# Scores of a 64-row head contracted over 128 rows, with each head's queries in zero-padded tiles of their own

## The chip, the cores and the metric

One Trainium2 chip; the kernel is one program on one of its cores. The metric is device time in microseconds of one execution, the median of several. The core's engines are named as in the profile: PE (TensorE matmul), PEld (TensorE weight load), DVE (VectorE), ACT (ScalarE), POOL (GpSimd) and SP (SyncE, which issues the transfers).

## The reference, cut to what matters

The model is one decoder layer over 512 tokens of width 1024: a half-step SwiGLU, a token mixing part, a cross-attention into 256 memory tokens, a second half-step SwiGLU, a final norm. The change lies in the token mixing part, whose mixer B is a causal attention with 8 heads of 64 channels, each query seeing keys by three strides:

```
q = z[..., o0:o0 + D_ATT].reshape(b, s, N_HEADS, HEAD_DIM)      # 8 heads of 64
k = z[..., o0 + D_ATT:o0 + 2 * D_ATT].reshape(b, s, N_HEADS, HEAD_DIM)
...
scores = jnp.einsum('bnqrhe,bnkrhe->bnrhqk', qb.astype(F32), kb.astype(F32)) * (e ** -0.5)
```

A score is a sum over the 64 channels of one head. Two heads fill the 128 rows of one tile.

## The kernel before, in words

All matrix products are made to float32 accuracy out of three products of a rounded half and a rest (`mm3`, lines 124 to 129: high by high on L127, high by low on L128, low by high on L129). So each operand exists as a pair of tiles, `...H` and `...L`, which `split` (L102 to L104) makes: ACT copies to the rounded tile (L103) and DVE subtracts (L104). Such pairs of 128 x 512 tiles come from one pool of 40 buffers (`h_tile`, L96). PSUM has four buffers for accumulators (`acc`) and four for everything short (`aux`).

In the mixing part (`mixers`, L389 on) the projections run as `z_block`, each 96 matmuls of 512 columns. Queries and keys come out with tokens on the rows; `qk_transpose` (L438) turns them with PE transposes (L442) into four tiles per call, two of queries and two of keys, and splits each to `qkH` and `qkL`. Tile m holds head 2m in rows 0 to 63 and head 2m+1 in rows 64 to 127. The call with b = 0 stands ahead of the last projection, the one with b = 1 in the middle of the attention.

The attention works on 32 units (tile m, half r, block i of 128 queries). For a unit u three functions are called at different steps: `scores(u)` (L491: one `mm3` on the 64 rows of the half r, over 256, 256, 384 or 512 keys, then DVE adds the mask and takes the maximum on L501, ACT takes the exponent on L505, DVE scales by the reciprocal sum on L508 and L509), `transposes(u - 3)` (L512: PE transposes on L517, then a split to the `pt` pair; one block of `pt` is zero-filled by POOL on L524), and `values(u - 4)` (L530: matmuls of `pt` by the value tiles, then ACT and DVE make `yH` and `yL`, L548 and L549). A unit of attention matmuls is short, so the work that the mixer's output projection can already do (`mix_out`, L607, part 0: 96 matmuls `acc<-yH` and `acc<-yL` on the other mixer's half) stands among the units as filler.

The order on each engine is not written out by hand: the program is traced, and a scheduler puts each engine's instructions in one fixed order by priorities and its own estimates. Engines keep that order and wait for each other by semaphores.

Of the kernel before, what the change touches and what calls it, by code (L numbers as in the profile page):

```python
# [24 lines left out]
P = 128  # L25
# [29 lines left out]
def body(tc, I, out):  # L55
    nc = tc.nc
    from contextlib import ExitStack
    ctx = ExitStack()
    with ctx:
# [22 lines left out]
        ps = paux.tile([P, S], F32, name="warm_ps", tag="aux")  # L82
# [10 lines left out]
        def aux_tile():  # L93
            return paux.tile([P, S], F32, name="aux", tag="aux")

        def h_tile(n):  # L96
            return hp.tile([P, S], F32R, name=n, tag="h")

        def f32(ap):
            return ap.bitcast(F32)  # L100

        def split(hi, lo, src):  # L102
            ins = nc.scalar.activation(hi, src, AF.Copy)  # L103
            nc.vector.tensor_sub(lo, src, f32(hi))  # L104
            return ins
# [14 lines left out]
        def at(x, i):  # L120

            return x[i[0]][i[1:]] if isinstance(x, list) and isinstance(i, tuple) else x[i]

        def mm3(ps, a, b, ia, ib, start, stop):
            aH, aL = at(a[0], ia), at(a[1], ia)
            bH, bL = at(b[0], ib), at(b[1], ib)
            nc.tensor.matmul(ps, lhsT=aH, rhs=bH, start=start, stop=False)  # L127
            nc.tensor.matmul(ps, lhsT=aH, rhs=bL, start=False, stop=False)  # L128
            nc.tensor.matmul(ps, lhsT=aL, rhs=bH, start=False, stop=stop)  # L129
# [259 lines left out]
        def mixers(norm, cs):  # L389
            col = []  # L390
            hshape = [P, 8, 64]
            with tc.tile_pool(name="mix", bufs=1) as mp:
# [43 lines left out]
                qT, kT = {}, {}  # L436

                def qk_transpose(b):  # L438
                    for m in range(4):
                        ps = aux_tile()  # L440
                        for t in range(NT):
                            nc.tensor.transpose(ps[:, t * P:(t + 1) * P],  # L442
                                                qk[t][:, m * P:(m + 1) * P], ident_b)
                        hi, lo = h_tile("qkH"), h_tile("qkL")
                        split(hi, lo, ps)
                        (qT if m < 2 else kT)[2 * b + m % 2] = (hi, lo)

                vH = [h_tile("vH") for _ in range(NT)]
                vL = [h_tile("vL") for _ in range(NT)]
# [7 lines left out]
                z_block(norm, 2, qk_evac)  # L457
                z_block(norm, 3, v_evac)
                qk_transpose(0)


# [14 lines left out]
                for t in range(NT):  # L476
                    vt = V[:, t].rearrange("p (g c) -> p g c", g=8)
                    r = rs[:, t * 8:(t + 1) * 8]
# [11 lines left out]

                def scores(u):  # L491
                    m, r, i = units[u]
                    rows = slice(r * 64, (r + 1) * 64)
                    n = (i + 1) * P
                    N = max(n, 256)
                    sc = aux_tile()
                    mm3(sc[:, :N], qT[m], kT[m], (rows, slice(i * P, (i + 1) * P)),
                        (rows, slice(0, N)), True, True)
                    s = mp.tile([P, S], F32, name="s", tag="s2", bufs=SB)
                    nmx = sm.tile([P, 1], F32, name="nmx", tag="nmx")  # L500
                    nc.vector.tensor_tensor_reduce(  # L501
                        out=s[:, :n], in0=sc[:, :n], in1=const[:, C_MASK + S - n:C_MASK + S],
                        scale=-ATT_SCALE, scalar=3e38, op0=ALU.add, op1=ALU.min, accum_out=nmx)
                    Z = sm.tile([P, 1], F32, name="Z", tag="Z")
                    nc.scalar.activation(s[:, :n], s[:, :n], AF.Exp, bias=nmx, scale=-1.0,  # L505
                                         accum_out=Z)
                    rz = sm.tile([P, 1], F32, name="rz", tag="rz")
                    nc.vector.reciprocal(rz, Z)  # L508
                    nc.vector.tensor_scalar_mul(s[:, :n], s[:, :n], rz)  # L509
                    prob[u] = s  # L510
# [80 lines left out]
                for u in range(LAG):  # L591
                    scores(u)
                z_block(norm, 4, qk_evac)
                gate_out()
                for u in range(LAG, nu + LAG + 1):
                    if u == nu // 2 - LAG - 1:
                        qk_transpose(1)
                    if u < nu:
                        scores(u)
                    transposes(u - LAG) if u - LAG < nu else None  # L600
                    if u > LAG:
                        values(u - LAG - 1)
# [281 lines left out]
```

## Time and profile before

| | |
|---|---|
| time, median of 3 runs | 1136.86 us (1136.83 to 1137.74) |
| the profiled execution | 1139.12 us |
| its span, first to last instruction | 1137.3 us |
| PE busy | 1121.1 us (99% of the span) |
| PEld busy | 936.4 us (82%) |
| DVE busy | 589.2 us (52%) |
| ACT busy | 422.6 us (37%) |
| POOL busy | 66.2 us (6%) |
| mean granted TensorE clock | 0.993 of full speed |
| stage with the scores | first score matmul at 468.7 us, last at 555.2 us |

PE is busy nearly throughout, so what a stage costs is mostly how closely its matmuls follow each other. A matmul's end is modelled in this profile and neighbours overlap on paper; the time that a matmul takes from the stream is the distance of its start from the next one's start. That distance, and not the duration shown, is used below.

### The profile page before, as it was taken

What the parts mean: (1) busy time and instruction counts of PE and PEld (TensorE: products, weight loads), DVE (VectorE), ACT (ScalarE), POOL (GpSimd) and SP (SyncE); (2) the same over time, 40 slices, a digit from 0 to 9 for tenths busy, and PEclk for the clock granted to TensorE, in tenths of its full rate; (3) what the DMA queues carried; (4) which work ended last, traced back from release to release, by engine and by line L of the source; (5) the groups of instructions that cost most, each with busy time, mean ns of one, the idle gap of its engine ahead of it and who ended that gap; (6) DMA issues with size and microseconds to landing.
All of it is one profiled execution on the core that took longest, in us unless ns stands there. A gap on an engine that the chain in (4) does not pass through costs nothing. (4 is left out here: it accounts for less than half of the span.)

```text
span 1137.3 us, 13932 instructions
## 1 busy us (share of the span) xinstructions
PE 1121.1 (99%) x5472; PEld 936.4 (82%) x5472; DVE 589.2 (52%) x1023; ACT 422.6 (37%) x668; POOL 66.2 (6%) x82
## 2 busy tenths in 40 slices
PE   9999999999999999999999999999999999999996
PEld 7788888888888888877868988778888888888996
DVE  4544533444344456578797555455444334445542
ACT  6332322332233433567655344433222222233420
POOL 2000100000002000001121000120000000000011
PEclk9999999999999999999989999999999999999998
DMA  6322333222233423010135412132232333323511
GB/s 218 112 93 88 114 97 128 93 93 94 83 88 114 141 93 108 25 45 29 41 111 196 165 63 74 47 102 93 95 99 75 89 125 97 108 93 113 154 63 38
DMA packets 39698, 110.79 MB, mean 97 GB/s; under 512 B 4432, under 2 KB 9296, under 8 KB 39632
## 3 DMA queue, kind: packets, MB, share of 16 engines
q1 hardware_dynamic: 39632, 109.89, 30.1%
q8 instruction: 43, 0.70, 0.2%
q14 instruction: 23, 0.19, 0.1%
HBM read 107.78 MB, written 2.10 MB: 97 GB/s over the span
## 5 line engine op out<-in xcount | busy, mean ns | idle before, releaser
L103 ACT ACTIVATE whi<-wraw 128x1024 fp32r<-128x1024 f32 (+2 forms) x213 | 202.8, 953 | 522.0 <-PE acc L128 300.9
L104 DVE TENSOR_TENSOR wlo<-wraw,whi 128x1024 fp32r<-128x1024 f32 (+2 forms) x213 | 238.4, 1120 | 166.7 <-ACT whi L103 166.4
L127 PE MATMUL acc<-hH,whi 128*128 128x512 f32 x768 | 300.8, 392 | 0.6 <-ACT hH L202 0.6
L128 PE MATMUL acc<-hL,whi 128*128 128x512 f32 x768 | 299.3, 390 | 0.8 <-DVE hL L203 0.8
L129 PE MATMUL acc<-hH,wlo 128*128 128x512 f32 x768 | 299.3, 390 | 0.5 <-DVE wlo L104 0.5
L128 PEld LDWEIGHTS acc<-hL,whi 128*128 128x128 f32 x768 | 144.3, 188 | 31.6 <-DVE hL L203 1.5
L127 PEld LDWEIGHTS acc<-hH,whi 128*128 128x128 f32 x768 | 144.3, 188 | 31.6 <-ACT hH L202 1.0
L129 PEld LDWEIGHTS acc<-hH,wlo 128*128 128x128 f32 x768 | 144.2, 188 | 30.6 <-DVE wlo L104 1.0
L127 PE MATMUL acc<-hidH,whi 128*128 128x512 f32 (+1 forms) x308 | 115.5, 375 | 0.0
L129 PE MATMUL acc<-hidH,wlo 128*128 128x512 f32 (+1 forms) x308 | 115.3, 374 | 0.0
L128 PE MATMUL acc<-hidL,whi 128*128 128x512 f32 (+1 forms) x308 | 115.3, 374 | 0.0
L170 POOL TENSOR_TENSOR sq<-sq 128x512 f32<-128x512 f32 (+1 forms) x39 | 49.3, 1265 | 778.8 <-ACT sq L178 778.4
L247 DVE TENSOR_TENSOR u<-acc,R 128x512 f32<-128x512 f32 x44 | 30.4, 690 | 121.6 <-PE acc L129 121.6
L243 DVE TENSOR_TENSOR gp<-acc,R 128x512 f32<-128x512 f32 x44 | 30.4, 691 | 85.6 <-PE acc L129 81.7
L128 PEld LDWEIGHTS acc<-hidL,whi 128*128 128x128 f32 x308 | 58.0, 188 | 10.3
L127 PEld LDWEIGHTS acc<-hidH,whi 128*128 128x128 f32 x308 | 58.0, 188 | 10.2
L129 PEld LDWEIGHTS acc<-hidH,wlo 128*128 128x128 f32 x308 | 58.0, 188 | 10.2
L127 PE MATMUL acc<-whi,hH 128*128 128x512 f32 x160 | 62.6, 391 | 0.0
L129 PE MATMUL acc<-whi,hL 128*128 128x512 f32 x160 | 62.4, 390 | 0.0
L128 PE MATMUL acc<-wlo,hH 128*128 128x512 f32 x160 | 62.3, 389 | 0.0
L230 DVE SCALAR_TENSOR_TENSOR x<-acc,x 128x512 f32<-128x512 f32 (+1 forms) x40 | 23.3, 584 | 75.0 <-PE acc L129 75.0
L178 ACT ACTIVATE sq<-x 128x512 f32<-128x512 f32 (+1 forms) x48 | 26.0, 551 | 41.8 <-DVE x L230 39.2
(211 smaller groups left out, 1476.6 us busy)
## 6 DMA issues: line engine op xcount, KB each, us to landing
wraw<-up SPq DMA_DIRECT2D x44, 512.0 KB, 3.5
wraw<-gate SPq DMA_DIRECT2D x43, 512.0 KB, 3.4
wraw<-down SPq DMA_DIRECT2D x28, 384.0 KB, 3.1
wraw<-w_in SPq DMA_DIRECT2D x20, 512.0 KB, 3.5
wraw<-down SPq DMA_DIRECT2D x28, 320.0 KB, 2.8
wraw<-w_out SPq DMA_DIRECT2D x16, 256.0 KB, 2.6
wraw<-wv SPq DMA_DIRECT2D x8, 512.0 KB, 3.4
wraw<-wk SPq DMA_DIRECT2D x8, 512.0 KB, 4.0
```

The costliest lines, as they stand in the source:

```text
L103: ins = nc.scalar.activation(hi, src, AF.Copy)
L104: nc.vector.tensor_sub(lo, src, f32(hi))
L127: nc.tensor.matmul(ps, lhsT=aH, rhs=bH, start=start, stop=False)
L128: nc.tensor.matmul(ps, lhsT=aH, rhs=bL, start=False, stop=False)
L129: nc.tensor.matmul(ps, lhsT=aL, rhs=bH, start=False, stop=stop)
L170: nc.gpsimd.tensor_add(self.parts[0], self.parts[0], sq)
L178: nc.scalar.activation(sq, src, AF.Square)
L230: nc.vector.scalar_tensor_tensor(X[d][:, tok], acc, 0.5, X[d][:, tok], op0=ALU.mult, op1=ALU.add)
L243: nc.vector.tensor_mul(gp, ps[0], R)
L247: nc.vector.tensor_mul(u, ps[1], R)
```

## The change

Keys stay as they are: two heads in one tile. Queries get, for each of the two heads, a pair of tiles of their own, whose other 64 rows POOL fills with zeros; ACT and DVE split only the head's own 64 rows into it. The score matmuls then take all 128 rows of the query tile and of the key tile; the rows of the other head meet zeros.

```
@@ -441,9 +441,21 @@
                         for t in range(NT):
                             nc.tensor.transpose(ps[:, t * P:(t + 1) * P],
                                                 qk[t][:, m * P:(m + 1) * P], ident_b)
-                        hi, lo = h_tile("qkH"), h_tile("qkL")
-                        split(hi, lo, ps)
-                        (qT if m < 2 else kT)[2 * b + m % 2] = (hi, lo)
+                        if m >= 2:
+                            hi, lo = h_tile("qkH"), h_tile("qkL")
+                            split(hi, lo, ps)
+                            kT[2 * b + m % 2] = (hi, lo)
+                            continue
+
+
+                        qT[2 * b + m % 2] = []
+                        for r in range(2):
+                            hi, lo = h_tile("qkH"), h_tile("qkL")
+                            rows, other = (slice(x * 64, (x + 1) * 64) for x in (r, 1 - r))
+                            for x in (hi, lo):
+                                nc.gpsimd.memset(f32(x[other]), 0.0)
+                            split(hi[rows], lo[rows], ps[rows])
+                            qT[2 * b + m % 2].append((hi, lo))
@@ -490,12 +502,11 @@
                 def scores(u):
                     m, r, i = units[u]
-                    rows = slice(r * 64, (r + 1) * 64)
                     n = (i + 1) * P
                     N = max(n, 256)
                     sc = aux_tile()
-                    mm3(sc[:, :N], qT[m], kT[m], (rows, slice(i * P, (i + 1) * P)),
-                        (rows, slice(0, N)), True, True)
+                    mm3(sc[:, :N], qT[m][r], kT[m], (slice(None), slice(i * P, (i + 1) * P)),
+                        (slice(None), slice(0, N)), True, True)
```

The number of matmuls stays the same; lines behind the first piece stand 12 lower, and behind the second 11 lower, in the changed kernel. Since the scheduler sees other instructions, its order moves. Three places matter.

POOL, from the last fill of the mixer's preparation on, before the change (`pt` is the zeroed block of a pair of transposed units, `sqb` the squares for the norm at the end):

```order
L524 MEMSET pt 128x128 x2
L170 TENSOR_TENSOR sq<-sq 128x512
L524 MEMSET pt 128x128 x18
L170 TENSOR_TENSOR sqb<-sqb 128x512
L524 MEMSET pt 128x128 x8
```

and now, from the same place (the eight fills `qkH` and `qkL` of the call with b = 0 stand between the `sq` and the first row shown here):

```order
L535 MEMSET pt 128x128 x4
L456 MEMSET qkH 64x512
L456 MEMSET qkL 64x512
L456 MEMSET qkH 64x512
L456 MEMSET qkL 64x512
L456 MEMSET qkH 64x512
L456 MEMSET qkL 64x512
L456 MEMSET qkH 64x512
L456 MEMSET qkL 64x512
L535 MEMSET pt 128x128 x14
```

Eight fills of the call with b = 1 stand between the sixth and the seventh `pt` fill, that is between the fills for units 4 and 5 and those for units 6 and 7 (each pair of `pt` fills serves two units).

DVE, at the call with b = 1 in the middle of the attention, before:

```order
L549 SCALAR_TENSOR_TENSOR yL<-aux,gains,yH 64x256
L104 TENSOR_TENSOR qkL<-aux,qkH 128x512 x2
L104 TENSOR_TENSOR wlo<-wraw,whi 128x512
L104 TENSOR_TENSOR qkL<-aux,qkH 128x512 x2
L501 ISA s,nmx<-aux,const 128x128
```

and now:

```order
L560 SCALAR_TENSOR_TENSOR yL<-aux,gains,yH 64x256
L104 TENSOR_TENSOR qkL<-aux,qkH 64x512 x2
L104 TENSOR_TENSOR qkL<-aux,qkH 128x512
L104 TENSOR_TENSOR qkL<-aux,qkH 64x512 x2
L104 TENSOR_TENSOR qkL<-aux,qkH 128x512
L512 ISA s,nmx<-aux,const 128x128
```

Four splits have become six, and the split of a weight tile that stood among them has moved elsewhere.

PE, from the last `values` matmul of the attention on, with buffer numbers (`acc` is an output tile of `mix_out`, `yH` one of its eight input tiles), before:

```order
L129 MATMUL aux_4499<-pt_4476,vL_2991 128x256
L129 MATMUL acc_4729<-yH_3638,wlo_4725 128x512
L127 MATMUL acc_4729<-yH_3647,whi_4724 128x512
L128 MATMUL acc_4729<-yL_3648,whi_4724 128x512
L129 MATMUL acc_4729<-yH_3647,wlo_4725 128x512
L127 MATMUL acc_4729<-yH_3656,whi_4724 128x512
```

and now:

```order
L129 MATMUL aux_4531<-pt_4508,vL_2991 128x256
L127 MATMUL acc_4781<-yH_3751,whi_4776 128x512
L128 MATMUL acc_4781<-yL_3752,whi_4776 128x512
L129 MATMUL acc_4781<-yH_3751,wlo_4777 128x512
L127 MATMUL acc_4781<-yH_4014,whi_4776 128x512
L128 MATMUL acc_4781<-yL_4015,whi_4776 128x512
```

Before, ten matmuls of part 0 of `mix_out` were left at this point; now part 1, which works on the attention's own output, begins right here, and all of part 0 stands among the units.

## Rows read from the trace of the kernel before

**Rows 1.** Busy time by stretch: us, then busy us of PE, PEld, DVE, ACT, POOL (instructions), clock, DMA share, GB/s.

```profile
460.00:488.00 28.00, 27.99 (x142) 22.85 (x141) 15.96 (x45) 15.17 (x31) 0.34 (x2) 1.00 0.11 37
488.00:566.00 78.00, 77.75 (x449) 60.16 (x448) 63.60 (x198) 53.20 (x139) 7.96 (x30) 1.00 0.09 26
566.00:600.00 34.00, 31.17 (x124) 24.20 (x123) 31.03 (x59) 18.48 (x30) 8.40 (x5) 0.90 0.39 125
```

**Rows 2.** Timeline of PE in two units: start us, us, engine, line, operation, xcount.

```profile
503.47 0.28 PE L128 MATMUL aux<-pt,vH 128*128 128x256 f32 x1
503.59 0.28 PE L129 MATMUL aux<-pt,vL 128*128 128x256 f32 x1
503.80 0.38 PE L127 MATMUL aux<-qkH 64*128 64x256 f32 x1
504.02 0.28 PE L128 MATMUL aux<-qkL,qkH 64*128 64x256 f32 x1
504.14 0.28 PE L129 MATMUL aux<-qkH,qkL 64*128 64x256 f32 x1
504.35 0.44 PE L517 MATMUL aux<-const,s 128*128 128x128 f32 x2
504.71 0.38 PE L127 MATMUL aux<-qkH 64*128 64x256 f32 x1
...
505.26 0.55 PE L517 MATMUL aux<-const,s 128*128 128x128 f32 x3
505.56 0.48 PE L129 MATMUL acc<-yH,wlo 128*128 128x512 f32 x1
505.88 0.40 PE L127 MATMUL acc<-yH,whi 128*128 128x512 f32 x1
506.11 0.40 PE L128 MATMUL acc<-yL,whi 128*128 128x512 f32 x1
...
508.34 0.66 PE L517 MATMUL aux<-const,s 128*128 128x128 f32 x4
508.93 0.49 PE L127 MATMUL aux<-qkH 64*128 64x512 f32 x1
...
509.50 0.39 PE L129 MATMUL aux<-qkH,qkL 64*128 64x512 f32 x1
509.82 0.50 PE L127 MATMUL acc<-yH,whi 128*128 128x512 f32 x1
510.15 0.39 PE L128 MATMUL acc<-yL,whi 128*128 128x512 f32 x1
```

**Rows 3.** All instructions of a kind: ns min/median/max, first and last start us, shapes.

```profile
L127 PE MATMUL aux<-qkH x32: 275/412/497, 468.7 to 554.6; 64*128 64x256 f32 x16, 64*128 64x384 f32 x8, 64*128 64x512 f32 x8
L104 DVE TENSOR_TENSOR qkL<-aux,qkH x8: 679/680/692, 463.8 to 516.6; 128x512 fp32r<-128x512 f32 x8
L127 PEld LDWEIGHTS aux<-pt,vH x48: 186/188/193, 497.6 to 565.5; 128*128 128x128 f32 x48
```

**Rows 4.** Costliest DVE groups, 488 to 566 us: busy us, mean ns | idle before them, what ended it.

```profile
L501 DVE CUSTOM_DVE_ANT_0 s<-aux,const 128x512 f32<-128x512 f32 (+3 forms) x29 | 14.2, 490 | 4.7 <-PE aux L129 4.6
L508 DVE RECIPROCAL rz<-Z 128x1 f32<-128x1 f32 x29 | 4.6, 158 | 2.2 <-ACT s L505 1.8
```

**Rows 5.** POOL's groups over the span, same columns.

```profile
L170 POOL TENSOR_TENSOR sq<-sq 128x512 f32<-128x512 f32 x27 | 40.0, 1481 | 428.3 <-ACT sq L178 427.9
L524 POOL MEMSET pt<- 128x128 f32 x32 | 6.2, 216 | 171.2 <-PE aux L128 140.3 <-PE aux L129 27.3 <-PE acc L129 3.6
L873 POOL MEMSET const-float32-0.0<- 128x1 f32 x1 | 0.1, 98 | 0.2 <-issue 0.2
```

**Rows 6.** Timeline of POOL during the first units: start us, us, xcount, idle before.

```profile
498.77 0.37 POOL L524 MEMSET pt<- 128x128 f32 x2 [27.31 <-PE aux L129]
503.81 0.38 POOL L524 MEMSET pt<- 128x128 f32 x2 [4.67 <-PE aux L128]
...
512.73 0.49 POOL L524 MEMSET pt<- 128x128 f32 x2 [4.71 <-PE aux L128]
```

## The prediction, as made before the run

> **What bounds the kernel now.** I read the busy time by stretch first. In the 78 us that hold 29 of the 32 units PE is busy for 77.75, at full clock; DVE is next with 63.60, ACT has 53.20 and POOL 7.96 [rows 1]. So PE sets the time there, and DVE has 14.4 us to spare. In the 34 us behind it the order turns round: DVE is busy for 31.03 and PE for 31.17 with a lower clock, so PE waits for DVE there. Then I read the timeline of PE for two units, by the distance from one start to the next [rows 2]. In the stream a 128-row matmul of 256 columns takes 0.12 us (503.47 to 503.59), one of 512 columns 0.23 (505.88 to 506.11). Inside a unit's three 64-row matmuls the last step is 0.12 as well (504.02 to 504.14), so 64 rows are no quicker than 128. But each border between the two kinds costs extra: the last 128-row matmul ahead of a unit takes 0.21 in place of 0.12 (503.59 to 503.80), and the first 64-row one 0.22 in place of 0.12. On the way out the last 64-row one takes 0.21 (504.14 to 504.35), or 0.32 in place of 0.23 at 512 columns (509.50 to 509.82), and the 128-row one behind it again 0.33 in place of 0.23. No row shows a wait there; these steps come at every border alike.
>
> **What the change removes.** The borders, all of them, since every matmul then has 128 rows. By kind:
> - Entry from a matmul: 0.09 + 0.10 = 0.19 us.
> - Entry from transposes: four transposes and the step to a 64-row matmul take 0.59 (508.34 to 508.93), two take 0.36 (504.35 to 504.71), so one more transpose costs 0.115. Three and the step to a 128-row matmul take 0.30 (505.26 to 505.56), so two would take about 0.18 where they take 0.36: 0.18 saved. The first matmul behind transposes is slow with 128 rows too (505.56 to 505.88 is 0.32 for 0.23), so its 0.10 stays.
> - Exit to a matmul: 0.09 + 0.10 = 0.19. Exit to transposes: 0.09, and about 0.05 in the first transpose (0.30 for three is 0.05 more than two times 0.115 and a step of 0.02), 0.14.
>
> In PE's order there are 32 runs of score matmuls, one for each of the 32 units [rows 3] on the whole (two units stand side by side, one is cut in two). 19 are entered from a matmul, 13 from transposes; 11 are left to a matmul, 21 to transposes. 19 x 0.19 + 13 x 0.18 + 11 x 0.19 + 21 x 0.14 = 3.6 + 2.3 + 2.1 + 2.9 = **11.0 us** off PE, 10.0 of it in the 78 us.
>
> **What it adds.**
> - Four ACT and four DVE splits more, two each per call. Nothing shows a 64 x 512 split; by its length it costs what the 128 x 512 one costs, 0.68 on DVE [rows 3], by its share of rows half. I take 0.68, since DVE's instructions run along the length, and it makes 1.4 us per call. The first call lies in the stretch where DVE is busy 15.96 of 28 us and PE has matmuls of the projection to go on with [rows 1]: nothing, at worst 1.4. The second goes to DVE's bill below.
> - 16 fills of 64 x 512 on POOL. A fill of one element takes 98 ns, one of 128 elements 216 [rows 5], so 0.92 ns an element and 0.57 us for 512; the upper end is POOL's add of that length, 1.48. The first eight stand in POOL's order ahead of the only `pt` fills between 460 and 488, where POOL is busy for 0.34 us [rows 1]: free. The second eight stand between two pairs of `pt` fills: behind the one at 498.77 and ahead of the one at 503.81 [rows 6]. They take 4.6 us, which is that gap. Even at 1.48, 11.8 us, they and the pair would be through at 511.4, and PE reads that pair's block only just ahead of 512.73, where the buffer is filled anew. I take nothing.
> - A fill beside DVE: the pair at 512.73 takes 0.49 us for the usual 0.37 or 0.38 [rows 6], so POOL is at times held up, and nothing shows DVE held up by a fill; I take nothing. The Trainium skill (SBUF — State Buffer, "Who interferes with whom") says that GpSimd and a VectorE instruction in a two-port mode shut each other out for a whole instruction, whichever comes second waiting; the longer fill at 512.73 agrees with it. By it each fill of the second eight could hold a scaling (L509) for up to 0.57; two or three of them fall into 4.6 us, and the sum below would be some 1.4 us smaller.
> - The ten matmuls of part 0 now ahead of the last values: 2.3 us at 0.23 each, moved from the stretch behind into the units.
>
> **What becomes late next: DVE.** The 78 us become 68 for PE, and 70.3 with the moved filler. DVE has 63.6, plus 1.4 for the splits, plus an output tile's add for the moved filler (not over 0.7, the price of a 512-long instruction), 65.7. Of its 14.4 idle us, the 4.7 ahead of L501 end with PE and shrink; the 2.2 ahead of L508 are the wait for its own unit's exponent on ACT and stay [rows 4]. That is 67.9, against 70.3 for PE with the moved filler: 97%. Two engines so nearly level that hand work to each other in fixed order lose something to each other; between 0 (PE alone counts) and all of the 10.0 (DVE keeps its 14.4 idle us: 65.7 + 14.4 = 80) I take 2.0, near the low end, because scores run three units ahead of their transposes and most of DVE's idle time now ends with PE or with ACT behind PE. Behind the units DVE is the bound (31.03 of 34 [rows 1]) and does the same work after the change, so PE's 2.3 us that left this stretch are given back only in part: I charge 1.0, between 0 and 2.3.
>
> **Sum.** 11.0 - 2.0 - 1.0 = 8.0 us. Against the profiled execution that is 1139.1 - 8.0 = 1131.1; the median of the runs stands 2.2 lower, at 1136.9, so **1128.9**.
>
> **Rivals.**
> - *PE's whole gain arrives.* DVE's idle time gives way fully: 1136.9 - 11.0 = 1125.9, and with what the coarse steps may have rounded off, 1125. For it: PE is the bound in the units now. Against: DVE at 97% of the new time in the units.
> - *DVE takes most of it.* It keeps half of its idle time or more: 65.7 + 10 is 76, and of the 78 us only 2 to 5 are left, 1132 to 1135; with all its idle time kept, nothing. For it: DVE's share of 82% and the stretch behind, where it is the bound already. Against: the 4.7 us that end with PE.
> - *It doesn't do what it says*: the extra steps belong to a change of operand or buffer, not of rows, and stay; DVE's splits then cost 0 to 1.4: 1137 to 1138. Against: the steps between matmuls of `acc` and of `pt`, with other operands and another buffer, show none of it, and the units' own matmuls among themselves neither.
> - *Slower: weight loads come out of cover.* Each matmul has a load of its own, 0.19 us for 128 rows [rows 3]. If the load of a 128-row score matmul could not run beside the matmul ahead of it, 96 of them would cost 18 us against the 11 saved: 1144. It decides from 0.115 us of exposed load per score matmul on (11.0 / 96). Against: the 128-row `pt` matmuls have such loads and start 0.12 apart [rows 2], less than one load takes. The Trainium skill (TensorE: Matmul & The Clock Gate, "The mechanism") says that a load overlaps a running matmul only where their row groups differ, which would bear this rival out; the rows of the `pt` matmuls here do not agree with it.
>
> **How the numbers follow.** Forecast, with 1126 to 1131.5 as its own range: 0.71. The whole gain, below 1126: 0.08. DVE takes most, 1131.5 to 1134.6: 0.10. DVE takes all, or the borders stay: 0.06. Slower by the loads or by a wait that I have not seen: 0.05. A change of under 0.2% (2.3 us) a measurement can't tell from none. So faster 0.71 + 0.08 + 0.10 = 0.89, same 0.06, slower 0.05. The range from 1125.0 to 1133.0 leaves out the last two, the upper half of DVE's case and a little at the bottom.
>
> **What would show it.** The 64-row forms are gone; the step into and out of a unit's matmuls is 0.12 and 0.23 like the stream's; `qkH` and `qkL` show 64 x 512 splits of 0.6 to 0.7 us; the last score matmul comes 7 to 9 us earlier; DVE's share among the units rises above 90%, and waits of PE for DVE (`pt`, `s`) appear there, where PE is now busy for all but 0.25 of 78 us. Steps of 0.2 that are still there would prove the first step wrong; PE gaps in the units of more than 4 us in all would prove the charge for DVE too small.

## The result, and the profile after

The change takes 1129.48 us (median, 1129.09 to 1130.39) where the kernel before takes 1137.54 beside it: a ratio of 0.9932 (95% interval 0.9921 to 0.9943), or 8.1 us (6.5 to 9.0). The forecast was 1128.9, 8.0 us under its own base. The profiled execution after the change took 1129.09 us with a span of 1127.3; PE is busy for 1110.1 us of it, DVE for 590.9, POOL for 74.3.

Busy time by stretch after the change, columns as in [rows 1], with the units' own 70 us (488 to 558) added:

```profile
460.00:488.00 28.00, 27.91 (x146) 23.64 (x145) 18.33 (x51) 16.86 (x34) 0.36 (x2) 1.00 0.12 38
566.00:600.00 34.00, 30.18 (x122) 23.53 (x121) 33.50 (x44) 20.56 (x30) 11.18 (x7) 0.95 0.43 141
488.00:558.00 70.00, 69.80 (x449) 59.65 (x448) 62.84 (x197) 54.08 (x141) 12.31 (x38) 1.00 0.10 31
```

PE now puts 449 matmuls into 70 us, as many as it put into 78 before [rows 1]. It shows 0.20 us idle there, and DVE has risen to 62.84 of 70, or 90%. Its timeline through two units, one of 384 and one of 512 columns (columns as in [rows 2]; the profile's L528 is the L517 of before):

```profile
504.20 0.28 PE L129 MATMUL aux<-pt,vL 128*128 128x256 f32 x1
504.32 0.34 PE L127 MATMUL aux<-qkH 128*128 128x384 f32 x1
504.50 0.34 PE L128 MATMUL aux<-qkL,qkH 128*128 128x384 f32 x1
504.67 0.34 PE L129 MATMUL aux<-qkH,qkL 128*128 128x384 f32 x1
504.85 0.60 PE L528 MATMUL aux<-const,s 128*128 128x128 f32 x4
505.20 0.48 PE L127 MATMUL aux<-qkH 128*128 128x512 f32 x1
505.51 0.40 PE L128 MATMUL aux<-qkL,qkH 128*128 128x512 f32 x1
505.75 0.40 PE L129 MATMUL aux<-qkH,qkL 128*128 128x512 f32 x1
505.98 0.40 PE L127 MATMUL acc<-yH,whi 128*128 128x512 f32 x1
506.22 0.39 PE L128 MATMUL acc<-yL,whi 128*128 128x512 f32 x1
```

The matmul ahead of the unit takes 0.12 us (504.20 to 504.32), not 0.21; the three scores step by 0.18, 0.17 and 0.18; four transposes and the step behind them take 0.35 (504.85 to 505.20) where [rows 2] had 0.59; the way out at 512 columns is 0.23 (505.75 to 505.98), where it was 0.32 and 0.33. Only the first matmul behind transposes is slow still (505.20 to 505.51), as forecast.

All instructions that touch `qkH`, columns as in [rows 3]:

```profile
L127 PEld LDWEIGHTS aux<-qkH x32: 186/190/193, 469.6 to 548.3; 128*128 128x128 f32 x32
L127 PE MATMUL aux<-qkH x32: 278/340/505, 469.9 to 548.3; 128*128 128x256 f32 x16, 128*128 128x384 f32 x8, 128*128 128x512 f32 x8
L104 DVE TENSOR_TENSOR qkL<-aux,qkH x12: 671/692/694, 463.6 to 513.7; 64x512 fp32r<-64x512 f32 x8, 128x512 fp32r<-128x512 f32 x4
L456 POOL MEMSET qkH<- x8: 519/523/721, 377.3 to 500.5; 64x512 f32 x8
```

The 64-row forms are gone. A 64 x 512 split costs DVE 0.69 us (0.68 was taken), and a fill costs POOL 0.52 (0.57 was taken). The eight fills of the second call, in POOL's timeline (columns as in [rows 6]):

```profile
497.31 0.52 POOL L456 MEMSET qkH<- 64x512 f32 x1
...
500.46 0.72 POOL L456 MEMSET qkH<- 64x512 f32 x1
501.13 0.52 POOL L456 MEMSET qkL<- 64x512 f32 x1
501.60 0.34 POOL L535 MEMSET pt<- 128x128 f32 x2
504.42 0.39 POOL L535 MEMSET pt<- 128x128 f32 x2 [2.48 <-PE aux L128]
```

They are through at 501.65, and POOL is idle again before the next `pt` fill: free, as forecast. PE's waits between 440 and 620 us (what was waited for, then total, times, longest, in us), after the change

```profile
PE acc L129 <- DVE wlo L104: 2.1, 1, 2.1
PE acc L127 <- DVE yo L630: 1.7, 1, 1.7
PE aux L127 <- DVE yL L597: 0.2, 1, 0.2
```

and before:

```profile
PE acc L129 <- DVE wlo L104: 2.1, 1, 2.1
PE acc L127 <- DVE yo L619: 0.6, 1, 0.6
```

The one wait that grew, by 1.1 us, lies behind the units: with ten filler matmuls fewer there, PE reaches an output tile sooner and waits for DVE to free it (`yo`).

**Where the time went**, by stretches between PE's own starts. From the first transpose of the first `qk_transpose` call (460.82 before, 460.59 after) to the last `values` matmul (565.88 and 558.55) it takes 105.06 us before and 97.96 after: 7.1 less, with ten fillers more (2.3 us). From there to the first matmul of `wv` it takes 32.39 before and 29.90 after, but 31.09 in a second profile of the kernel before (the last experiment), so 1.2 of the 2.3 come back. What is left lies outside. The step of one filler, a 512-column matmul, is taken as 0.233 us here and below.

### The profile page after: what moved, and what is told of

The parts are those of the page before. It is cut to its first block, busy times and chain, and to the rows that moved or that the text cites. A ratio compares the mean times of both kernels' runs of the same rounds, so it can differ in the third digit from the quotient of the medians.

```text
span 1127.3 us, 13958 instructions
## 1 busy us (share of the span) xinstructions
PE 1110.1 (98%) x5472; PEld 934.7 (83%) x5472; DVE 590.9 (52%) x1027; ACT 425.0 (38%) x672; POOL 74.3 (7%) x98
```

## The experiments

**1. The score matmuls back on 64 rows, all else as after the change.** The tiles, splits, fills and the order on PE stay the same.

```
-mm3(sc[:, :N], qT[m][r], kT[m], (slice(None), slice(i * P, (i + 1) * P)),
-    (slice(None), slice(0, N)), True, True)
+rows = slice(r * 64, (r + 1) * 64)
+mm3(sc[:, :N], qT[m][r], kT[m], (rows, slice(i * P, (i + 1) * P)),
+    (rows, slice(0, N)), True, True)
```

> The changed kernel with the score matmuls cut back to the head's own 64 rows of the padded tiles. All splits, fills and the order of every engine stay those of the changed kernel; only the row count of 96 matmuls goes back. Theory (the borders between 64-row and 128-row matmuls cost 11 us on PE): the borders return and PE's 1.5 us of waits for DVE and ACT in the units go, so 1129.5 + 11.0 - 1.5 = 1139, that is 1 to 2 us over the kernel before, and the steps of 0.2 us show again at each border. Rival (the gain came from the new order of the instructions): 1129.5, as the changed kernel. Second rival (64-row weight loads or matmuls save something elsewhere): below 1137.

Measured: 1139.41, ratio to before 1.0018 (1.0009 to 1.0026). PE's timeline at a unit of 256 columns (L529: the transposes):

```profile
503.72 0.28 PE L129 MATMUL aux<-pt,vL 128*128 128x256 f32 x1
503.93 0.38 PE L127 MATMUL aux<-qkH 64*128 64x256 f32 x1
504.15 0.28 PE L128 MATMUL aux<-qkL,qkH 64*128 64x256 f32 x1
504.27 0.28 PE L129 MATMUL aux<-qkH,qkL 64*128 64x256 f32 x1
504.47 0.44 PE L529 MATMUL aux<-const,s 128*128 128x128 f32 x2
```

The steps of 0.21, 0.22, 0.12 and 0.20 of the kernel before are back, in the tiles and the order of the change. So they belong to the rows, not to an operand or a buffer, and at the same order their absence is worth 1139.41 - 1129.48 = 9.9 us. In the stretch of the units it is 107.84 - 97.96 = 9.9 too, and since both traces have one order, they can be compared step by step: with 128 rows the steps at the borders (the one ahead of a unit's scores, the scores' own and the one behind them) are 10.6 us shorter in sum, and all the others 0.7 longer. The second thing that this run says: additions and order, without the gain, cost 2.1 us over before (1.0 to 3.0).

**2. One of three on 64 rows.** Is the price one per matmul of 64 rows, or one per border?

```
+nc.tensor.matmul(sc[:, :N], lhsT=qh[:, c], rhs=kh[:, 0:N], start=True, stop=False)
+nc.tensor.matmul(sc[:, :N], lhsT=qh[:, c], rhs=kl[:, 0:N], start=False, stop=False)
+nc.tensor.matmul(sc[:, :N], lhsT=ql[rows, c], rhs=kh[rows, 0:N], start=False, stop=True)
```

> The changed kernel with only the third of a unit's three score matmuls on 64 rows, the other two on 128; order as in the changed kernel. There are then as many borders as in the kernel before (32 in, 32 out) but a third of the 64-row matmuls. Theory (borders cost, by their number): about the same as with all three on 64 rows, 1138 to 1139.5. Rival (each 64-row matmul is slow in itself, whatever stands beside it): a third of the way from the changed kernel, 1129.5 + 3 = 1132.5.

Measured: 1139.92, ratio 1.0022 (1.0013 to 1.0031), the same as with all three on 64 rows, and 0.4 over the theory's range. In the timeline (L510 to L512 are the three matmuls) the border has only moved inward, and entry and exit fall on one matmul, 0.31 for its 0.12:

```profile
503.34 0.28 PE L510 MATMUL aux<-qkH 128*128 128x256 f32 x1
503.46 0.28 PE L511 MATMUL aux<-qkL,qkH 128*128 128x256 f32 x1
503.67 0.38 PE L512 MATMUL aux<-qkH,qkL 64*128 64x256 f32 x1
503.98 0.44 PE L531 MATMUL aux<-const,s 128*128 128x128 f32 x2
```

**3. Twice the borders.** The first and third of three on 64 rows, the second on 128 between them; the order on PE is that of experiment 1, but for the first two of the three, which change places.

```
+nc.tensor.matmul(sc[:, :N], lhsT=qh[rows, c], rhs=kl[rows, 0:N], start=True, stop=False)
+nc.tensor.matmul(sc[:, :N], lhsT=qh[:, c], rhs=kh[:, 0:N], start=False, stop=False)
+nc.tensor.matmul(sc[:, :N], lhsT=ql[rows, c], rhs=kh[rows, 0:N], start=False, stop=True)
```

> The changed kernel with the first and the third of a unit's score matmuls on 64 rows and the second between them on 128 (the product of high by low is put first for it, the work is the same). Twice the borders of the kernel before, 64 in and 64 out, with two thirds of its 64-row matmuls. Theory (each border has its price): 32 more ways in and 32 more ways out between matmuls at 0.19 us each, 12 us over the run with one of three on 64 rows, 1151 to 1152. Rival (a unit with 64-row matmuls pays once, however they are mixed): 1140, as the runs with one or three of three on 64 rows.

Measured: 1151.26, ratio 1.0125 (1.0109 to 1.0140): 14.3 us over before, where experiment 1 stood 2.1 over it. Two borders more in each of 32 units cost 12.2 us, or 0.19 each, which is the price that [rows 2] gave for a border between matmuls. One such unit:

```profile
505.64 0.28 PE L129 MATMUL aux<-pt,vL 128*128 128x256 f32 x1
505.85 0.38 PE L510 MATMUL aux<-qkL,qkH 64*128 64x256 f32 x1
506.16 0.39 PE L511 MATMUL aux<-qkH 128*128 128x256 f32 x1
506.47 0.38 PE L512 MATMUL aux<-qkH,qkL 64*128 64x256 f32 x1
506.79 0.44 PE L531 MATMUL aux<-const,s 128*128 128x128 f32 x2
```

**4. Only the rows.** The kernel before in its own order, with the score matmuls over all rows of the undivided tiles.

```
-mm3(sc[:, :N], qT[m], kT[m], (rows, slice(i * P, (i + 1) * P)), (rows, slice(0, N)), True, True)
+mm3(sc[:, :N], qT[m], kT[m], (slice(None), slice(i * P, (i + 1) * P)),
+    (slice(None), slice(0, N)), True, True)
```

> The kernel before with its score matmuls over all 128 rows of the undivided query and key tiles: no splits, fills or tiles added, and the order of every engine that of the kernel before. It leaves out the separation of the heads (each score is the sum over two heads), so it shows the borders' removal by itself. Theory: 1137.5 - 11 = 1126.5, or up to 1.5 more where DVE, which then has 65 of 67 us in the units, holds PE up; 1 to 3 us below the changed kernel, which is the price of what the change adds. Rival (the added splits and fills are all hidden): 1129.5 as the changed kernel. Rival (the gain is the new order's): 1137.

Measured: 1128.89, ratio 0.9920 (0.9906 to 0.9933), 8.4 us under before: not told apart from the change itself. The stretch of the units takes 96.24 us. Before's 105.06 less the 11.0 of the borders would be 94.1, so 2.2 us come back with no split, fill or filler added: the steps at the borders are 10.7 us shorter than before the change, and the others 1.8 longer. The two longest of these are 0.35 and 0.34 more, each ahead of a unit pair's first `values` matmul, for which ACT's square (`sqb`) of an earlier pair frees a PSUM buffer; in the profile only part of the step shows as idle:

```profile
528.82 0.40 PE L127 MATMUL acc<-yH,whi 128*128 128x512 f32 x1
529.40 0.36 PE L127 MATMUL aux<-pt,vH 128*128 128x256 f32 x1 [0.18 <-ACT sqb L551]
```

The whole 11 does not arrive in before's order either. The time is 0.9 over the theory's range and nearest to the first rival, that what the change adds is hidden; the second, that the gain is the new order's, is out.

**5. Less work for DVE.** The scaling of the scores by the reciprocal sum (the L509 of before, L520 after the change) is left out, the only edit.

```
-nc.vector.tensor_scalar_mul(s[:, :n], s[:, :n], rz)
```

> The changed kernel without the scaling of the 32 score tiles by the reciprocal sums (it leaves the division of the softmax out). DVE has 11 us less work among the units, and the scheduler's order moves a little. Theory (after the change DVE is as full as PE in the units, which costs PE 1.5 to 2 us of waits): 1127.5 to 1128.3, and PE's waits in the units nearly gone. Rival (DVE is not in PE's way; the missing part was a wrong price of the borders): 1129.5.

Measured: 1129.46, ratio 0.9927 (0.9914 to 0.9939): nothing gained. Busy time from 488 to 544 us after the change

```profile
488.00:544.00 56.00, 55.80 (x358) 47.81 (x357) 51.52 (x164) 44.48 (x116) 9.91 (x31) 1.00 0.10 29
```

and without the scaling:

```profile
488.00:544.00 56.00, 55.79 (x365) 47.80 (x364) 46.15 (x149) 46.20 (x124) 11.19 (x36) 1.00 0.08 25
```

DVE fell from 92% to 82% of the stretch, and PE got only seven more matmuls into it. The stretch of the units takes 93.22 us with 73 fillers in it, where the change has 97.96 with 96 and before has 86. Before's 105.06, less 11.0, less 13 fillers at 0.233 (3.0), is 91.0: 2.2 us lost in small waits, not fewer than after the change (1.6, worked out below). What the fillers made shorter among the units came back behind them, in a `wv` stage of 24.5 us in place of 21.1 (first to last start), where PE's longest wait between 440 and 640 us is 2.7, for `wlo`. So nothing here says that DVE's throughput holds the units, though the order moved with the edit.

**6. Squares once per tile.** The ACT square per pair of units (16 in all, not 15) goes, and one square per finished `yH` tile takes its place.

```
-nc.scalar.activation(sqs[m][rows, c], o, AF.Square)
 if r == 1 and i == NT - 1:
+    nc.scalar.activation(sqs[m], f32(yH[4 + m]), AF.Square)
```

> The changed kernel with the squares of the attention's output taken once per tile from the rounded, scaled copy at the end of a tile, in place of 15 times from the PSUM buffer of the values (it leaves out that the norm is of the unscaled output, and the rest part of it). ACT has about 4 us less to do and the PSUM buffer is free one ACT instruction earlier. Theory (PE's small waits among the units, some 1.5 us more than in the kernel before, are waits for a PSUM buffer that these squares free last, and not for DVE's throughput): 1127.5 to 1128.5. Rival (they pass on to the next reader of the buffer, or the order that the scheduler makes sets them): 1129.5.

Measured: 1133.32, ratio 0.9966 (0.9953 to 0.9978), a miss: 3.8 us slower than the change. The units' stretch, 96.45 us with 93 fillers, holds 0.8 us of waits by the same working. But the scheduler's order changed with the edit, and PE waits behind the units for one weight tile:

```profile
PE acc L129 <- DVE wlo L104: 7.2, 1, 7.2
```

About half of that wait is DVE held up beside POOL: of the four DVE instructions from 577.62 to 583.79, the last of which is the split waited for, three take 1.74 to 1.75 us in place of 0.68 to 0.75 and one 1.17, 3.6 us in all, while POOL adds squares (575.44 to 583.24); ahead of the wait for `wlo` after the change it is 1.4. The profile then holds 6.8 us at half clock, where the change's holds 3.4. So the time of that run is set behind the units, and what the squares cost among them it leaves open.

**7 and 8. Weight rests on POOL.** In 7 the rest of each `w_out` tile is subtracted on POOL, and in 8 those of the memory tiles too.

```
-last["hi"] = split(hi[:, p], lo[:, p], raw[:, p])
+if sub is None:
+    last["hi"] = split(hi[:, p], lo[:, p], raw[:, p])
+else:
+    last["hi"] = nc.scalar.activation(hi[:, p], raw[:, p], AF.Copy)
+    sub(lo[:, p], raw[:, p], f32(hi[:, p]))
...
+w = load_weight(I["w_out"][part, d], [4, P], sub=nc.gpsimd.tensor_sub)
```

> The changed kernel with the rest part of the 16 weight tiles of the mixer's output projection subtracted on POOL in place of DVE. DVE loses some 12 us of work, half of it behind the units, POOL gains 16 instructions of about 1.5 us. Theory (behind the units DVE is the bound: PE waits 1.7 + 2.1 us for it there and then runs 3.4 us at half clock, 5.5 us in all): 1124.5 to 1127. Rival (POOL's result comes 0.8 us later for each tile, and its reads hold up DVE's additions of two SBUF tiles): 1129 to 1133.

> As the run with the rest part of the output projection's weights on POOL, and the rest part of the four memory tiles on POOL too, which takes another 2.8 us off DVE behind the units. Theory (DVE is the bound there): 1 to 2 us below that run. Rival (POOL, with its own additions of squares there, is now the late one): the same as that run or slower.

Measured: 1131.51 (ratio 0.9948, 0.9936 to 0.9961) and 1133.62 (0.9969, 0.9956 to 0.9981). DVE's busy time from 488 to 558 fell to 60.29 and 60.40 from 62.84, and neither is faster than the change: 8 is slower, and the interval of 7 overlaps the change's at its edge. PE's idle time in that stretch rose from 0.20 to 1.67 and 1.78. In both PE waits for a small DVE operation behind the units that it did not wait for before; in 7 it is

```profile
PE aux L157 <- DVE dg L155: 2.1, 1, 2.1
```

and in 8 the same wait is 3.5 us. The trace shows where it comes from. On the way to `dg` stand DVE instructions of 128 x 4 that take 0.16 us; in 7 two of them take 1.26 and 1.23, each beside one of POOL's new subtractions, which is 2.2 us for a wait of 2.1:

```profile
562.42 1.26 DVE L147 SCALAR_TENSOR_TENSOR rcolby<-rcolbt,rcolby 128x4 f32<-128x4 f32 x1
564.88 1.23 DVE L146 SCALAR_TENSOR_TENSOR rcolbt<-rcolbt,rcolbv 128x4 f32<-128x4 f32 x1
```

```profile
562.29 1.37 POOL L121 TENSOR_TENSOR wlo<-wraw,whi 128x512 fp32r<-128x512 f32 x1 [2.81 <-ACT whi L120]
564.66 1.44 POOL L121 TENSOR_TENSOR wlo<-wraw,whi 128x512 fp32r<-128x512 f32 x1 [0.99 <-ACT whi L120]
```

In 8 it is four in a row (0.66, 1.22, 1.18 and 1.19 us), 3.6 for a wait of 3.5. That is 7's rival, DVE held up by POOL, on smaller instructions than it named. So these two runs do not say what less load on DVE is worth: much of what was taken off it came back as longer instructions.

**9. The queries split once, POOL makes the second pair.**

```
+both = h_tile("qkH"), h_tile("qkL")
+first = h_tile("qkH"), h_tile("qkL")
+for x in first:
+    nc.gpsimd.memset(f32(x[64:128]), 0.0)
+split(both[0], both[1], ps)
+for x, y in zip(first, both):
+    nc.gpsimd.tensor_copy(x[0:64], f32(y[0:64]))
+    nc.gpsimd.memset(f32(y[0:64]), 0.0)
```

> The queries are split once per tile pair, as before the change (four ACT and four DVE splits fewer than after it); POOL copies the upper head's or lower head's 64 rows into the second, zero-filled pair and fills the vacated rows with zeros. Theory: the second split per tile is a good part of the 2.1 us that the change's additions and order cost, and POOL's time is free: 1127.5 to 1129. Rival: POOL's copies stand between the split and the first score matmuls, and arrive late: a wait of PE for POOL at the first units and 1129.5 to 1133. Rival two: the additions' cost is one of order and not of the splits, 1129 to 1130.5, with no wait for POOL.

Measured: 1130.62, ratio 0.9941 (0.9928 to 0.9955), not told apart from the change. PE waits nowhere for POOL, and the wait for `wlo` behind the units grew from 2.1 to 3.2 us. So the run gives no sign that the change pays for its four added splits; since the order moved again (91 fillers among the units for 96), it does not price them either.

**10. The kernel before, profiled a second time.**

> The kernel before, unchanged, with a second profile. Theory: the 10.0 us between the two profiled executions and the 8.1 us between the medians differ because the first profile of the kernel before held 6.9 us at the half clock behind the units, where other kernels' profiles held 3.4: a second profile has 3.4 us of it and a span of 1135 to 1136. Rival: the 6.9 us belong to this kernel's order of work, and come again with a span of 1137.3.

Measured: span 1136.3, 1.0 less than the first profile, 0.3 over the theory's range. Windows just behind the units, first profile (the clock stands behind POOL's column):

```profile
588.00:592.00 4.00, 3.56 (x8) 2.81 (x9) 4.00 (x6) 1.69 (x3) 1.58 (x1) 0.50 0.42 131
592.00:596.00 4.00, 4.00 (x13) 3.15 (x12) 3.45 (x5) 2.34 (x5) 1.64 (x2) 0.67 0.74 262
```

and second:

```profile
588.00:592.00 4.00, 3.35 (x11) 2.63 (x12) 4.00 (x5) 1.69 (x4) 1.59 (x1) 0.76 0.41 131
592.00:596.00 4.00, 4.00 (x16) 3.21 (x15) 3.97 (x6) 2.68 (x5) 1.66 (x2) 0.81 0.75 262
```

Behind PE's short idle time the granted clock falls to half, 1.2 for 2.4 GHz, for 6.8 us in the first profile (587.8 to 594.7) and for 3.4 in the second (590.1 to 593.5). The stretch from the last `values` matmul to `wv` is 1.3 us longer in the first (32.39 and 31.09), the span 1.0, and so much of the distance between the profiled spans of before and after goes with it. The 3.4 that the expectation gives for other kernels does not hold for all: the change and 1, 2, 4, 7 and 9 held 3.4, but 3, 6 and 8 held 6.8, and 5 none there.

## Why the prediction was right

- **Borders, 11.0 us off PE.** Right, price and mechanism. The steps came back with the 64 rows in the change's own tiles and order (experiment 1, 9.9 us net), went by the number of borders and not of 64-row matmuls (2), and cost 0.19 each when they were doubled (3). The count of 11.0 was made in before's order, and there the steps at the borders shrank by 10.7 (4). Of the 1.1 us between 11.0 and 9.9, 0.7 are other steps that became longer; the remaining 0.4 stand in the border steps, part of it waits (the one at 497.61 below).
- **No exposed weight loads.** The slow rival named loads of 0.19 us. They are there (190 ns in the rows of `qkH`), and 128-row score matmuls of 384 columns start 0.17 to 0.18 apart, and those of 256 columns of experiment 2 start 0.12 apart (503.34 to 503.46), all the same. The rule of the Trainium skill (TensorE: Matmul & The Clock Gate, "The mechanism"), that a load overlaps only a matmul of other row groups, does not agree with these rows; they would fit what the same section says besides, that a load into the background weight buffer is pulled ahead too.
- **Additions, nothing.** Right in the sizes (0.69 and 0.52 us for 0.68 and 0.57), and right that POOL hides the fills. Experiment 9 gives no sign that the splits are a price either. Of the two scalings beside the second eight fills one was held up a little (0.48 us at 497.97 for 256 columns, which take 0.33 to 0.36 elsewhere, with a fill from 497.78 to 498.30) and one was not (0.41 at 500.31 for 384 columns). So of the 1.4 us by the other rule of the Trainium skill (SBUF — State Buffer, "Who interferes with whom") 0.1 fell due there. That it was so little is a matter of timing: in experiment 1, with the same order, two scalings beside the fills took 0.74 for 0.35 and 0.63 for 0.41.
- **The charge of 2.0 among the units: size near, cause not as said.** 105.06 - 11.0 + 2.3 would be 96.4; the stretch took 97.96, so 1.6 us are lost. The step took 2.0 out of a range of 0 to 10.0, and that it came so near is partly luck: it said that the loss comes from DVE at 97% of PE's time, DVE stands at 90%, and with ten points less PE loses as much (experiment 5). Of the 1.6, 0.5 are there without the gain (107.84 - 105.06 - 2.3, experiment 1). The rest comes along with the faster PE, as do the 2.2 us in before's own order (4). Where the traces name what ends it, it is mostly a single wait for a buffer that another engine still reads, and such waits hide in steps more than in idle time: four transposes from 497.03 and the step behind them take 0.58 us, where those from 504.85 take 0.35, and the score matmul at 497.61 starts just as DVE's split of `pt` (0.55 us from 497.00) ends. In experiment 4 it is ACT's squares that end the longest ones. How the loss divides between DVE and ACT, no run here settles.
- **The charge of 1.0 behind the units.** Right. 1.2 of 2.3 us come back, so 1.1 are lost, and it is one wait: the one for `yo`, from 0.6 to 1.7 us, with DVE busy for 33.50 of the 34 us from 566.
- **Signs.** DVE's share "above 90%" came out at 89.8%. The last score matmul came 6.3 us earlier and not 7 to 9, since the first came 1.2 later. Waits of PE for DVE did not appear as idle time among the units, 0.20 us in all. DVE's wait for its unit's exponent did not stay at 2.2 [rows 4]; ahead of the reciprocal (now L519) it is 1.5, and ahead of the maximum (now L512) 0.9 for 4.7:

```profile
L512 DVE CUSTOM_DVE_ANT_0 s<-aux,const 128x512 f32<-128x512 f32 (+3 forms) x29 | 14.1, 487 | 0.9 <-PE aux L129 0.7
...
L519 DVE RECIPROCAL rz<-Z 128x1 f32<-128x1 f32 x29 | 4.6, 157 | 1.5 <-ACT s L516 1.4
```

- **Base.** The profiles differ by 10.0 us and the medians by 8.1. One us of it is the longer half clock in the first profile of before (experiment 10); the profile after was also the fastest of its five executions. Setting the sum against the profiled execution and then taking the 2.2 us off to the median was the right way round.

## What to carry to other kernels

Where matmuls of 64 and 128 rows stand in one stream, count the borders and not the short matmuls, and read their price from the distance of starts, since the profile calls none of it idle: here 64 rows saved no time and each border cost 0.14 to 0.19 us, so zeros in the other rows were the cheaper way. When the bounding engine gets faster by a tenth, part of it is given back in small waits and in a stage behind that another engine holds, here a quarter of 11 us, even where nothing was added (4). Taking load off the engine that looks next in line is worth testing before it is believed: three such edits here gave nothing or lost up to 4 us. In one (5) the order moved with the edit; in the two that moved the work to POOL, POOL held up DVE's other instructions.

## What the runs showed that was not expected

- The same kernel, in the same order and with the same wait ahead of it (2.09 us for `wlo`), ran 6.8 us at half clock in one profile and 3.4 in the next. Without the scaling (experiment 5) PE waited 2.7 us for `wlo` at 588 us, and the clock stayed full. A profiled span can be a microsecond long by that alone.
- DVE instructions run long beside POOL. After the change a scaling (`s`, 128 x 128, L520) took 0.97 us at 530.80 for its usual 0.28 while POOL added two squares (1.28 us from 530.12), and the next DVE instruction follows at 531.62, after POOL's end at 531.40. It is not alone. Measured against the median of their kind over all runs, 20 DVE instructions after the change take over 0.15 us too long, 15.0 us in all, and 20 before it with 15.2; every one of them, in every run, overlaps a POOL instruction. In 7 it is 29 with 22.2 us, in 8 33 with 24.2. Five of the 20, 3.4 us, lie between the last `values` matmul and `wv`, where DVE is busy nearly throughout. What that costs PE there was not tested: no run takes POOL's additions away.
